# Product-key experts on Trainium2: gates of the listed experts made in list order instead of gathered

## The chip, the cores and the metric

The kernel runs on one core of a Trainium2 chip. A core has TensorE (matrix products, reading SBUF, writing PSUM banks), VectorE, ScalarE and GpSimd for elementwise work, and queues that issue DMA transfers: SyncE's (SP), ScalarE's, and GpSimd's, which issues the indirect ones (row gathers). Each engine runs its own instructions in order and waits on semaphores for the others. The metric is the time of one execution on the device in microseconds (us). The kernel before took 1694.18 us, the median of three runs (1691.24 to 1699.25).

## The reference, cut to what matters

One decoder layer: two kinds of attention, then the expert layer (PEER), then a gated embedding, each followed by a layer norm. The change touches the expert layer only. There are 256 tokens of width 2048, 16,384 experts (numbered ia x 128 + ib), and 8 heads that choose 16 experts each for every token:

```python
cand = (va[..., :, None] + vb[..., None, :]).reshape(t, PEER_HEADS, PEER_TOPK * PEER_TOPK)
cidx = (ia[..., :, None] * PEER_NKEYS + ib[..., None, :]).reshape(...)
top, sel = lax.top_k(cand, PEER_TOPK)
eidx = jnp.take_along_axis(cidx, sel, axis=-1)
gates = jax.nn.softmax(top, axis=-1)
...
    ub = u[eb]
    vbk = v[eb]
    act = jax.nn.gelu(jnp.einsum('thed,td->the', ub, xb).astype(jnp.float32))
    w = (gb * act).astype(xb.dtype)
    return jnp.einsum('the,thed->td', w, vbk)
```

So each token has 128 entries (8 heads x 16), an entry being an expert (ia, ib) with a gate.

## The kernel before, in words

**Sparse and dense tokens.** The first 88 tokens (NSP) are "sparse": for each, the u and the v row of each of its 128 experts is gathered, 176 gathers of 128 rows (1 MB), and VectorE forms the dot products (L1006) and the weighted sums (L1016), in `sparse_work`. The other 168 (NDT) are "dense": for them TensorE multiplies blocks of 128 experts with all tokens at once, and a weight matrix [expert, token] that is zero nearly everywhere holds gate times gelu.

**Two parts of the experts.** Rows ia 0 to 55 (SEG1) are the first part: their u rows are loaded whole in 56 blocks (`u_block`), and gelu of the products stands in A0 and A1, [ib, ia, token]. Rows ia 56 to 127 (SEG2 = 72) are the second part. `list_work` makes for each part a list of the experts that a dense token really uses, in blocks of 128: 24 + 15 = 39 blocks for the first, 30 + 18 = 48 for the second. The first 30 (24) blocks hold experts that only tokens 128 to 255 use (128 columns), the others all 168 columns. The lists are kept as row numbers `idxV` (rows of u and v) and `idxW` (rows of the stored weights). For the second part the u rows are gathered by list (`rows_of`), turned on TensorE (`rows_T`) and multiplied (`rows_mm`): gelu goes to WL, in list order. This is the loop over 48 u blocks.

**The gates.** `gate_work` takes three dense tokens (GB) at a time. VectorE makes two one-hots by `equal` (L714): `ohb` [entry, 128 values of ib] and `eq` [entry, ia]; ScalarE multiplies `eq` by the gate's upper half (`hi`, L1099), VectorE by its lower half (`lo`, L1101). TensorE multiplies `ohb` by `hi` and by `lo` (L1111, L1112): the result in a PSUM bank `ps_G` is the gate of each (ib, ia) for one token. VectorE scales it into place: for the first part into A0 and A1 by multiplication (L1125), for the second as plain gates into the buffer G2 (L1122). `gate_work` is a generator: the loops call `run(work, n)` to let it issue n steps between their own blocks (one step after one-hots, one after products). When all tokens are done, the weights go to DRAM by SP's queue (L289): `s_w0` for the first part, `s_w1` for the second. Row 0 of each is zero, for empty places of the list. The second part's gates begin at the 44th u block and end among the v blocks.

**The v blocks.** `v_fetch` gathers for each listed block two things on GpSimd's queue (L1329): `wc`, the stored weights of its 128 experts (672 bytes a row), and `vf`, their v rows (1 MB). For the second part `weigh` (L1434) multiplies the gathered gates by WL on VectorE. Then 16 products `v_mm` (L1411; an f32 product is two records in the trace) add to six PSUM banks. `vf` has the five slots of the pool `wf` (WF), the same as the u rows had, and `fetched` runs up to four blocks ahead (LEAD). Order: the 39 blocks of the first part, with `half` running two steps of `gate_work` after each half block; then 45 of the second, the last three (STAG) held back and done bank by bank with the layer norm's start. Before the last three a branch `rest` handles experts that didn't fit the lists; it isn't run when all fit.

**Paces.** `gathers(n)` lets `sparse_work` issue n sparse gathers on average after each block: GUL = (1.00, 1.40) after a u block of 128 or 168 columns, GV = (0.66, 0.95) after a v block. Most instructions off TensorE are kept in program order (`keep`); each engine's queue is therefore shared by blocks, gates and sparse sums in the order of issue.

Of the kernel before, what the change touches and what calls it, by code (L numbers as in the profile page):

```python
# [19 lines left out]
P = 128  # L20
# [48 lines left out]
GUL, GV = (1.00, 1.40), (0.66, 0.95)  # L69
# [6 lines left out]
STAG, LEAD, NWC = 3, 4, 8  # L76
# [92 lines left out]
def build(tc, a, out):  # L169
# [464 lines left out]
    m16 = gin.tile([P, 2, P], F16, name="m16")  # L634
    left = gin.tile([P, NIA], F32, name="left")
# [28 lines left out]
    niaT = tkl.tile([P, T], F32, name="niaT")  # L664
    nibT = tkl.tile([P, P], F32, name="nibT")
    zrow = tkl.tile([1, NDT], F32, name="zrow")
    nc.gpsimd.memset(zrow, 0.0)
    for i in range(2):
        nc.gpsimd.dma_start(a[f"s_w{i}"][0:1], zrow[:, None, :].to_broadcast([1, PARTS[i][1], NDT]))
# [180 lines left out]
    def index_T(t):  # L850

        c = slice(t * P, (t + 1) * P)
        for src, dst, neg in ((iaN, iaT, niaT[:, c]), (ibN, ibT, None if t else nibT)):
# [3 lines left out]
            if neg is not None:  # L857
                nc.scalar.mul(neg, ps[:, :P], -1.0)
# [18 lines left out]
    def act_one_hot(dst, pool, neg):  # L877

        d = pool.tile([P, P], F16, name="dist", tag="dist", bufs=1)
        nc.scalar.activation(d, io128, AF.Abs, bias=neg)  # L880
        nc.scalar.activation(dst, d, AF.Relu, bias=1.0, scale=-1.0)
# [6 lines left out]
    def first_flags():  # L888
# [5 lines left out]
        for t0 in range(NSP, P, GB):  # L894
            n = min(GB, P - t0)
            oa, ob = (tkl.tile([P, GB, P], F16, name=nm, tag=nm) for nm in ("oa", "ob"))
            for j in range(n):
                act_one_hot(oa[:, j, :], tkl, niaT[:, t0 + j:t0 + j + 1])
                act_one_hot(ob[:, j, :], tkl, nibT[:, t0 + j:t0 + j + 1])
# [5 lines left out]
    def second_flags(gating, flags):  # L905
# [8 lines left out]
        load(lin, a["c_lin"])  # L914
        iaC = flp.tile([P, SEGX, 2], F16, name="iaC")
# [9 lines left out]
        for i, t0 in enumerate(range(P, T, GB)):  # L925
# [3 lines left out]
            if i % 2:  # L929
                for j in range(n):  # L930
                    act_one_hot(eq[:, j, :], flp, niaT[:, t0 + j:t0 + j + 1])
# [152 lines left out]
    def gate_work(oh, parts, s0, ns, part, fresh):  # L1084

        def one_hot(t0, n):  # L1090
            ohb = oh.tile([P, GB, P], F16, name="ohb", tag="ohb", bufs=OHB)
            eq = oh.tile([P, GB, ns], F16, name="eq", tag="eq", bufs=OHB)
            hi = oh.tile([P, GB, ns], F16, name="hi", tag="hi", bufs=OHB)
            lo = oh.tile([P, GB, ns], F16, name="lo", tag="lo", bufs=OHB)
            equal(eq[:, :n], io128[:, s0:s0 + ns], iaT[:, t0:t0 + n])
            equal(ohb[:, :n], io128, ibT[:, t0:t0 + n])
# [10 lines left out]
        def product(t0, n, ohb, hi, lo):  # L1107
            ps = pbank(pa, "ps_G")
# [4 lines left out]
            return ps  # L1113

        def scale(t0, n, ps):
            g = ps[:, :n * ns].rearrange("p (t a) -> p a t", t=n)
            c0 = 0
            for At in parts:
                dst = At[:, :, t0 - NSP:t0 - NSP + n]
                c1 = c0 + At.shape[1]  # L1120
                if fresh:
# [814 lines left out]
```

## Time and profile before

| | before |
|---|---|
| median of 3 runs | 1694.18 us (1691.24 to 1699.25) |
| the profiled execution | 1699.17 us, its span 1697.4 us |
| instructions | 29309 |
| busy: TensorE matmul, VectorE, ScalarE, GpSimd | 1608.6, 1041.8, 723.3, 697.4 us |
| mean granted TensorE clock | 0.98 of full speed |
| moved by DMA | 528.49 MB, 311 GB/s over the span |

The profile is of one execution. It has the busy time of each engine, the same in stretches of the span, groups of instructions by line (with the idle time ahead of them and what ended it), waits (who waited for whom), and a timeline. A row such as `out<-in` names tiles of the program. "idle before" is the engine's idle time just before an instruction, put down to the event that came last. Matmuls are pipelined, so one's length in the trace is longer than the step from one to the next.

### The profile page before, as it was taken

Reading aid. Unit: us, or ns where it says so; the run is one execution under the profiler, and the core shown is the slowest. Engines: PE = TensorE matmul, PEld = TensorE weight load, DVE = VectorE, ACT = ScalarE, POOL = GpSimd, SP = SyncE. Lnnn points to the kernel's source line nnn. Section 1 sums busy time; section 2 is a strip of 40 time slices with the busy share of each in tenths; the row PEclk is TensorE's granted clock in tenths of the full one; section 3 lists DMA queues with packets and bytes.
Section 4 is the critical chain, followed back from the end, with each engine's and each line's share of the span. In section 5 each row is a group of like instructions: output and inputs, shape, how many; then the busy total and the mean of one; then the engine's idle time right before and its main releaser. Section 6 shows DMA issues by size and latency. Waiting matters only on the chain. (4 is left out here: it accounts for less than half of the span.)

```text
span 1697.4 us, 29309 instructions
## 1 busy us (share of the span) xinstructions
PE 1608.6 (95%) x11162; PEld 1485.0 (87%) x11162; DVE 1041.8 (61%) x2216; ACT 723.3 (43%) x1684; POOL 697.4 (41%) x586
## 2 busy tenths in 40 slices
PE   9999999999999899999999999899977988889998
PEld 7888888877889899999999999889867988889786
DVE  5555488763387897667576666378732444441776
ACT  5677468753111467856366665343300000000542
POOL 0134023202233434211556555448867878862000
PEclk9999999999999999999999999899998999999999
DMA  8544644484997799999899999999998999986561
GB/s 295 193 160 160 237 162 149 153 321 148 332 390 321 300 412 418 370 376 363 345 421 381 358 362 372 367 365 356 394 400 344 401 420 415 414 355 235 183 257 50
DMA packets 93658, 528.49 MB, mean 311 GB/s; under 512 B 13166, under 2 KB 16559, under 8 KB 41371
## 3 DMA queue, kind: packets, MB, share of 16 engines
q0 software_dynamic: 50320, 335.01, 50.2%
q1 hardware_dynamic: 41462, 188.40, 30.1%
q10 hardware_dynamic: 1728, 3.15, 0.5%
q8 instruction: 89, 1.46, 0.3%
q14 instruction: 59, 0.48, 0.1%
HBM read 512.60 MB, written 16.08 MB: 311 GB/s over the span
## 5 line engine op out<-in xcount | busy, mean ns | idle before, releaser
L1411 PE MATMUL ps_v<-wc,vf 128*128 128x128 f32 (+1 forms) x2784 | 373.3, 294 | 51.6 <-DMA vf<-v_rows,idxV 29.3
L1411 PEld LDWEIGHTS ps_v<-wc,vf 128*128 128x128 f32 x2784 | 360.6, 196 | 59.1 <-issue 24.6
L130 DVE TENSOR_TENSOR wl<-wf,wh 128x1024 fp32r<-128x1024 f32 (+1 forms) x199 | 212.7, 1092 | 121.5 <-ACT wh L129 120.0
L1016 DVE SCALAR_TENSOR_TENSOR y<-gb,ew,y 128x2048 f32<-128x2048 f32 x78 | 183.1, 2348 | 167.7 <-DMA gb<-v_rows,eig 167.6
L129 ACT CAST wh<-wf 128x1024 fp32r<-128x1024 f32 (+1 forms) x199 | 172.1, 892 | 267.2 <-DMA wf<-ple_gate 153.3
L220 PE MATMUL ps_u<-XF,wf 128*128 128x168 f32 x1632 | 250.7, 310 | 0.0
L220 PEld LDWEIGHTS ps_u<-XF,wf 128*128 128x128 f32 x1632 | 235.2, 191 | 3.1 <-issue 0.2
L1368 PE MATMUL ps_u<-XF,uT 128*128 128x128 f32 (+1 forms) x1536 | 226.1, 292 | 0.4 <-ACT uT L1362 0.4
L1006 DVE SCALAR_TENSOR_TENSOR gb<-gb,xq 128x2048 f32<-128x2048 f32 x88 | 200.7, 2285 | 31.6 <-DMA gb<-u_rows,eig 30.3
L1040 POOL DMA_INDIRECT gb<-u_rows,eig x88 | 119.6, 1360 | 215.2 <-DVE eqb L714 54.9
L1368 PEld LDWEIGHTS ps_u<-XF,uT 128*128 128x128 f32 x1536 | 203.2, 194 | 1.0 <-ACT uT L1362 0.7
L208 PE MATMUL ps_qk<-X,wh 128*128 128x512 f32 x512 | 185.2, 401 | 0.0
L1040 POOL DMA_INDIRECT gb<-v_rows,eig x88 | 148.1, 1683 | 44.0 <-issue 17.9
L1362 ACT COPY uT<-ps_T 128x512 f32<-128x512 f32 x192 | 111.6, 586 | 98.8 <-PE ps_T L1359 95.7
L210 PE MATMUL ps_qk<-X,wl 128*128 128x256 f32 x512 | 145.7, 285 | 0.0
L1329 POOL DMA_INDIRECT wc<-s_w,idxW x87 | 119.1, 1369 | 47.7 <-issue 22.9
L1099 ACT ACTIVATE hi<-eq,ghf 128x56 f16<-128x56 f16 (+1 forms) x336 | 92.3, 339 | 81.8 <-DVE eq L714 79.9
L1329 POOL DMA_INDIRECT vf<-v_rows,idxV x87 | 103.9, 1194 | 53.9 <-PE ps_v L1411 23.7
L220 PE MATMUL ps_q<-XF,wf 128*128 128x256 f32 x512 | 115.7, 384 | 1.1 <-ACT eb L589 1.1
L208 PEld LDWEIGHTS ps_qk<-X,wh 128*128 128x128 f32 x512 | 96.4, 188 | 22.0 <-issue 1.0
L1359 PE MATMUL ps_T<-ident,uf 128*128 128x128 f32 x768 | 115.5, 276 | 0.0
L1329 POOL DMA_INDIRECT uf<-u_rows,idxV x48 | 68.4, 1426 | 100.4 <-PE ps_T L1359 92.6
(345 smaller groups left out, 2498.4 us busy)
## 6 DMA issues: line engine op xcount, KB each, us to landing
wf<-peer_u SPq DMA_DIRECT2D x51, 1024.0 KB
wf<-w_qk SPq DMA_DIRECT2D x64, 512.0 KB
wf<-w_out SPq DMA_DIRECT2D x32, 512.0 KB
wf<-peer_wq SPq DMA_DIRECT2D x16, 1024.0 KB
wf<-ple_gate SPq DMA_DIRECT2D x16, 1024.0 KB
wf<-w_v SPq DMA_DIRECT2D x16, 512.0 KB
wf<-w_sv SPq DMA_DIRECT2D x15, 512.0 KB
s_w<-G SPq DMA_DIRECT2D x9, 672.0 KB
```

What stands on the lines that cost most here:

```text
L129: self.order(nc.scalar.copy(wh, src))
L130: self.order(nc.vector.tensor_tensor(wl, src, wh.bitcast(F32), op=ALU.subtract))
L208: nc.tensor.matmul(ps, wh[:, j * P:(j + 1) * P], xt[:, dt, :], start=dt == 0, stop=False)
L210: nc.tensor.matmul(ps[:, :T], wl[:, j * P:(j + 1) * P], xt[:, dt, :T], start=False, stop=dt == ND - 1)
L220: nc.tensor.matmul(ps[:, :T - t0], wf[:, dt * P:(dt + 1) * P], xt[:, dt, t0:], start=dt == 0, stop=dt == ND - 1)
L1006: keep(nc.vector.scalar_tensor_tensor(g, g, 1.0, xq[i], op0=ALU.mult, op1=ALU.mult, accum_out=eact[i][:, j:j + 1]))
L1016: keep(nc.vector.scalar_tensor_tensor(ys[i], g, ew[i][:, j:j + 1], ys[i], op0=ALU.mult, op1=ALU.add))
L1040: keep(nc.gpsimd.indirect_dma_start(out=g, out_offset=None, in_=a[kind], in_offset=bass.IndirectOffsetOnAxis(ap=eig[i][:, 0, j:j + 1], axi ...
L1329: keep(nc.gpsimd.indirect_dma_start(out=dst, out_offset=None, in_=src, in_offset=bass.IndirectOffsetOnAxis(ap=idx[:, b:b + 1], axis=0), bo ...
L1359: nc.tensor.transpose(ps[:, j * P:(j + 1) * P], uf[:, (4 * c + j) * P:(4 * c + j + 1) * P], ident)
L1368: nc.tensor.matmul(ps[:, :n], uT[:, j * P:(j + 1) * P], XF[:, d, NSP + c0:NSP + c0 + n], start=d == 0, stop=d == ND - 1)
L1411: return nc.tensor.matmul(o, vf[:, d * P:(d + 1) * P], wc[:, c0:c0 + n], start=False, stop=last and (d % 3 == 2 or d == ND - 1))
```

## The change

The second part's gates are not made in (ib, ia) order, stored and gathered; they are made directly in list order and multiplied into WL, where gelu stands.

- While `gate_work` makes the first part's gates, it also looks up, for all 128 entries of the three tokens, their place in the second part's list. TensorE turns the one-hot `ohb` (one product with a unit matrix, 128 columns, into a bank `ps_turn`), ScalarE copies it to SBUF as f16, and TensorE multiplies it with two small tables `maps` [ib, ia] of block number and place in the block (72 columns each). That gives [entry, ia]; VectorE picks the entry's own ia by comparing with `iaF` and summing (`pick`, one instruction with an accumulator for each token). `decode` splits the place into block and row.
- A second pass of `gate_work` uses row and block in place of ib and ia: 40 tokens with the 18 blocks of 168 columns, then 128 tokens with all 48 blocks, scaled by multiplication into WL. It is run beside the first part's v blocks, and nothing of it beside the u blocks; after the first part's store no step is run there.
- G2, its store `s_w1`, the 48 gathers of `wc` and `weigh` are gone: a v block of the second part multiplies with WL directly.
- Four more slots for v rows (`vx`, NVX) stand where G2 was; every second block among the first eight of a round of nine uses one, for the first part only. `ahead` is 8 blocks until the first part's last five are fetched, then 4 again.
- Paces: GUL (1.10, 1.50), GV (0.62, 0.88).
- The branch `rest` makes the gates of the second part itself (`expert_gates`), from four small tensors stored after the first part's v blocks.

```diff
-GUL, GV = (1.00, 1.40), (0.66, 0.95)
+GUL, GV = (1.10, 1.50), (0.62, 0.88)
...
+    maps = gin.tile([P, 2, SEG2], F16, name="maps")
+    ident16 = gin.tile([P, P], F16, name="ident16")
...
-        for t0 in list(range(NSP, T, GB)) + [None] * OHB:
...
+        made, multiplied, turned, picked = [], None, [], None
+        todo = [(t0, min(GB, t1 - t0), s0, ns, dsts) for first, t1, s0, ns, dsts in runs
+                for t0 in range(first, t1, GB)]
+        for group in todo + [None] * (OHB + 2 * (look is not None)):
+            if group is not None:
+                made.append((group, one_hot(*group[:4])))
             if multiplied:
-                scale(*multiplied)
+                (t0, n, s0, ns, dsts), ps = multiplied
+                scale(t0, n, ns, dsts, ps)
                 multiplied = None
+            if turned and len(turned[-1]) == 3:
+                t0, n, ps = turned.pop()
+                oht = oh.tile([P, GB * P], F16, name="oht", tag="oht", bufs=4)
+                keep(nc.scalar.copy(oht[:, :n * P], ps[:, :n * P]))
+                turned.append((t0, n, oht, True))
+            if picked:
+                look.pick(*picked)
+                picked = None
             yield
...
+            ps = pbank(pa, "ps_G")
+            if ready:
+                group, tiles = made.pop(0)
+                t0, n, _, ns, _ = group
+                product(ps, n, ns, *tiles)
+                multiplied = group, ps
+            if look is not None:
+                if len(turned) > 1 or not ready:
+                    t1, n1, oht, _ = turned.pop(0)
+                    o = ps[:, GB * SEG1:]
+                    look.find(t1, n1, oht, o)
+                    picked = t1, n1, o
+                if ready:
+                    pst = pbank(pa, "ps_turn")
+                    for j in range(n):
+                        nc.tensor.matmul(pst[:, j * P:(j + 1) * P], tiles[0][:, j, :], ident16,
+                                         start=True, stop=True)
+                    turned.append((t0, n, pst))
+            yield
...
+        def find(self, t0, n, oht, ps):
+            for j in range(n):
+                o = ps[:, j * SEG2:(j + 1) * SEG2]
+                for k in range(2):
+                    nc.tensor.matmul(o, oht[:, j * P:(j + 1) * P], maps[:, k], start=not k,
+                                     stop=k == 1)
+
+        def pick(self, t0, n, ps):
+            for j in range(n):
+                junk = self.oh.tile([P, SEG2], F16, name="junk", tag="junk", bufs=2)
+                keep(nc.vector.scalar_tensor_tensor(
+                    junk, io128[:, SEG1:], iaF[:, t0 + j:t0 + j + 1],
+                    ps[:, j * SEG2:(j + 1) * SEG2], op0=ALU.is_equal, op1=ALU.mult,
+                    accum_out=self.pos[:, t0 + j:t0 + j + 1]))
...
+    def all_gates(oh, A0, A1, WL):
+
+        places = Places(lkp, oh)
+        yield from gate_work(oh, iaT, ibT, [(NSP, T, 0, SEG1, ((A0, NSP), (A1, NSP)))], places)
...
+        nonlocal stored
+        stored = True
+        aT, bT = places.decode()
+        yield
+        nA, nB = CAPS[1]
+        WA = WL[:, :nA * P].rearrange("p (b t) -> p b t", t=P)
+        WB = WL[:, nA * P:].rearrange("p (b t) -> p b t", t=NDT)
+        yield from gate_work(oh, aT, bT, [(NSP, P, nA, nB, ((WB, NSP),)),
+                                          (P, T, 0, nA + nB, ((WA, P), (WB, NSP)))])
...
+        k = taken % (WF + NVX)
+        taken += 1
+        if k % 2 and k < 2 * NVX and not i and b < NBLK[0] - WF:
+            vf = vxp.tile([P, D], F32, name="vx", tag="vx", bufs=NVX)
+        else:
+            vf = slot("vf")
+        if i:
+            w = WL_of(b)
+        else:
...
+            rows_of(w, a["s_w"].rearrange("p a t -> (p a) t"), idxW[i], b)
...
-        if b == NBLK[1] - 5:
-            while not run(work, 1):
-                pass
+        if b == NBLK[1] - LEAD:
+            assert stored
             pools.close("a1p", "a0p")
-            g2p = pools.open("g2p", "right", bufs=1)
-            G2 = g2p.tile([P, SEG2, NDT], F32, name="G2")
+            vxp = pools.open("vxp", "right", bufs=1)
             wcp = pools.open("wcp", "right", bufs=1)
-            work = gate_work(ohp, (G2,), *PARTS[1], 1, True)
...
-            if b >= 2 and (c or n > P):
+            if b >= 2 and (c or n > P) and not stored:
                 run(work, 1)
...
-            while order and len(fetched) <= LEAD and (not order[0][0] or done):
-                fetch(wpool)
-            fetched[:3] = [weigh(block) for block in fetched[:3]]
-            i, b, vf, wc, _ = fetched.pop(0)
+            while order and len(fetched) <= (ahead if order[0] < (0, NBLK[0] - WF) else LEAD):
+                fetch()
+            block = fetched.pop(0)
```

More of the change, by code (lines that the diff above doesn't have):

```diff
@@ L856, in index_T @@
             nc.scalar.copy(dst[:, c], ps[:, :P, None].to_broadcast([P, P, 2]))
-            if neg is not None:
-                nc.scalar.mul(neg, ps[:, :P], -1.0)
+            if flat is not None:
+                nc.scalar.copy(flat, ps[:, :P])
             yield
@@ L1105, in one_hot, with product @@
             return ohb, hi, lo
-        def product(t0, n, ohb, hi, lo):
-            ps = pbank(pa, "ps_G")
+        def product(ps, n, ns, ohb, hi, lo):
             for j in range(n):
@@ L1142, in gate_work @@
-        if multiplied:
-            scale(*multiplied)
+            if turned and len(turned[-1]) == 3:
[6 more added lines that the diff above has]
+                picked = None
+            yield
+            ready = made and (len(made) > OHB - 2 or group is None)
@@ L1262, in list_work @@
         idxV[part] = iv
-        idxW[part] = iw
     def run(work, n):
@@ L1460, in build @@
         if b == NBLK[0] - LEAD:
-            while not done:
-                done = run(work, 1)
             more = nc.values_load(total[0:1, 0:1], min_val=0, max_val=NIA * NKEY)
-        v_blocks(1, wcp, half)
-    pools.close("ohp")
-    wcq = pools.open("wcq", "left", bufs=1)
+        v_blocks(1, LEAD + NVX, half)
+    assert done
+    for dst, src in zip(("s_ia", "s_ib", "s_gl"), (iaT, ibT, gl2)):
+        load(a[dst], src[:, NSP:])
+    load(a["s_gh"], ghf[:, NSP:])
+    pools.close("ohp", "lkp")
     for _ in range(LEAD + 1):
-        v_blocks(1, wcq)
-    pools.close("wcp", "g2p", "lsp")
+        v_blocks(1, LEAD)
+    pools.close("wcp", "vxp", "lsp")
     l2 = pools.open("l2", "right", bufs=1)
@@ L1535, in build, with expert_gates @@
         if b == N1 - STAG - 1:
-            fetched[:] = [weigh(block) for block in fetched]
             while not run(sparse, 1):
                 pass
+    def expert_gates(ia0, ia2, ib2, gl, gh):
+        G = spare[2][:, :FBC * NDT].rearrange("p (a t) -> p a t", t=NDT)
+        for t0 in range(0, NDT, 8):
+            t = slice(t0, t0 + 8)
+            eq, hi, lo = (fbp.tile([P, 8, FBC], F16, name=nm, tag=nm) for nm in ("e_", "h_", "l_"))
+            ohb = fbp.tile([P, 8, P], F16, name="o_", tag="o_")
+            equal(eq, io128[:, ia0:ia0 + FBC], ia2[:, t])
+            equal(ohb, io128, ib2[:, t])
+            shape = [P, 8, FBC]
+            keep(nc.vector.tensor_tensor(hi, eq, gh[:, t, None].to_broadcast(shape), op=ALU.mult))
+            keep(nc.vector.tensor_tensor(lo, eq, gl[:, t, 0:1].to_broadcast(shape), op=ALU.mult))
+            ps = pbank(pa, "ps_g")
+            for j in range(8):
+                for k, x in enumerate((hi, lo)):
+                    keep(nc.tensor.matmul(ps[:, j * FBC:(j + 1) * FBC], ohb[:, j], x[:, j],
+                                          start=not k, stop=k == 1))
+            keep(nc.vector.tensor_scalar(
+                G[:, :, t], ps[:, :8 * FBC].rearrange("p (t a) -> p a t", t=8), 1.0 / GSCALE,
+                None, op0=ALU.mult))
+        return G
@@ L1561, in build @@
     pools.close("fbp")
-    held = [weigh(block)[:4] for block in fetched]
+    held = list(fetched)
     assert len(held) == STAG and not order
```

168 lines of the change are left out of this document (93 added, 75 removed).

## The prediction

> **What bounds the kernel now.** I read the stages first, by the busy time in stretches of the span. The columns are the stretch, its length, the busy time of TensorE matmul, weight load, VectorE, ScalarE and GpSimd with instruction counts, then granted clock, DMA share and GB/s.
>
> ```profile
> core 0: us, PE busy (x) PEld busy (x) DVE busy (x) ACT busy (x) POOL busy (x), PEclk, DMA share, GB/s
> ...
> 846.00:1049.00 203.00, 203.00 (x1992) 201.76 (x1988) 135.45 (x330) 126.45 (x343) 119.51 (x72) 1.00 0.97 378
> 1049.00:1085.00 36.00, 36.00 (x275) 35.87 (x274) 13.11 (x8) 14.96 (x29) 12.27 (x10) 1.00 1.01 415
> 1085.00:1135.00 50.00, 39.98 (x281) 37.76 (x280) 33.34 (x59) 20.52 (x61) 30.50 (x21) 0.83 0.91 361
> 1135.00:1241.00 106.00, 101.72 (x1057) 98.78 (x1056) 79.08 (x193) 36.83 (x132) 80.81 (x57) 1.00 0.94 359
> 1241.00:1346.00 105.00, 81.84 (x518) 79.88 (x517) 33.38 (x16) 0.00 (x0) 75.25 (x56) 0.90 0.95 384
> 1346.00:1480.00 134.00, 114.60 (x977) 111.20 (x977) 56.81 (x56) 4.43 (x8) 106.62 (x78) 1.00 1.01 415
> 1480.00:1517.00 37.00, 29.87 (x203) 28.78 (x202) 20.90 (x25) 0.00 (x0) 28.15 (x22) 0.97 1.02 415
> 1517.00:1556.00 39.00, 38.72 (x256) 38.48 (x257) 2.67 (x9) 0.00 (x0) 9.63 (x11) 0.95 0.65 229
> ```
>
> The second part's u blocks run from 828 to 1135, the v blocks from 1135 to 1556: 39 of the first part until 1346, then 45 of the second. While gates are made beside u blocks (846 to 1049), TensorE never idles: it is the bound, VectorE is at two thirds. In the v blocks TensorE is idle for 24 us of 1241 to 1346 and 26 of 1346 to 1517, with the DMA share at 0.95 to 1.02: there the transfers bind. Only after 1517 is TensorE the bound again. The waits of TensorE between 840 and 1560 (total, times, longest) say for what:
>
> ```profile
> PE ps_v L1411 <- DMA vf<-v_rows,idxV: 29.3, 15, 8.6
> PE ps_v L1411 <- DVE wc L1434: 13.2, 7, 7.1
> PE ps_G L1111 <- ACT hi L1099: 9.6, 2, 5.9
> ```
>
> The second wait is the product of gate and value in gathered rows (`weigh`), the third the first gates of the second part. Both go with the change. The timeline of TensorE shows where, and the rates that the sum needs (start, length, operation, count, idle before):
>
> ```profile
> 1094.84 0.22 PE L1111 MATMUL ps_G<-hi,ohb 128*128 128x72 f16 x1 [5.88 <-ACT hi L1099]
> ...
> 1095.80 2.61 PE L1368 MATMUL ps_u<-XF,uT 128*128 128x168 f32 x8 [0.19 <-ACT uT L1362]
> ...
> 1109.35 0.22 PE L1111 MATMUL ps_G<-hi,ohb 128*128 128x72 f16 x1 [3.76 <-ACT hi L1099]
> ...
> 1125.93 1.31 PE L1368 MATMUL ps_u<-XF,uT 128*128 128x168 f32 x8
> ...
> 1139.64 0.20 PE L1111 MATMUL ps_G<-hi,ohb 128*128 128x72 f16 x1
> 1139.67 0.20 PE L1112 MATMUL ps_G<-lo,ohb 128*128 128x72 f16 x1
> ...
> 1139.84 2.03 PE L1411 MATMUL ps_v<-wc,vf 128*128 128x128 f32 x16
> 1141.70 0.20 PE L1111 MATMUL ps_G<-hi,ohb 128*128 128x72 f16 x1
> ```
> ```profile
> 1310.41 34.15 PE L1411 MATMUL ps_v<-wc,vf 128*128 128x168 f32 x224 [8.60 <-DMA vf<-v_rows,idxV]
> ...
> 1516.78 38.95 PE L1411 MATMUL ps_v<-wc,vf 128*128 128x168 f32 x256 [7.05 <-DVE wc L1434]
> ```
>
> An f32 matmul leaves two records, so a v block is 32 of them. 16 records and a gate group take 2.06 us (1139.64 to 1141.70): a 128-column v block with two groups costs 4.12 us, and without the two groups' twelve products at 31 ns about 3.7. A 168-column block costs 38.95 / 8 = 4.87.
>
> **Part 1: u blocks beside the gates and the lookup.** Per token the change adds one f16 matmul of 128 columns (the turn of the one-hot) and two of 72 (the lookup). The 72-column ones lie 31 ns apart above. For 128 columns no f16 row stands; by columns it is 55 ns, between 31 and the 127 ns of one f32 record (2.03 / 16). 168 x 0.055 + 336 x 0.031 = 19.7 us (bounds 15.6 to 32), all on the path, since TensorE is full there. Products of the second part made before 1135 leave this stage: nine or ten groups of six at 31 ns, 1.8 us. Their two stalls leave too: 5.88 + 3.76 us idle, and the slow matmuls behind them, for eight took 2.61 at 1095.80 and 1.31 at 1125.93 (clock 0.83 in that stretch). Four such octets and the transposes between them make some 5 us: 14 us in all.
>
> What ended these stalls on ScalarE was VectorE, whose one-hots stood behind the sparse sums. So VectorE must be costed (mean ns and idle before, in 846 to 1049):
>
> ```profile
> L1016 DVE SCALAR_TENSOR_TENSOR y<-gb,ew,y 128x2048 f32<-128x2048 f32 x15 | 35.2, 2348 | 1.6 <-DMA gb<-v_rows,eig 1.5
> L1125 DVE SCALAR_TENSOR_TENSOR A<-ps_G,A 128x18 f32<-128x18 f32 x111 | 23.4, 253 | 59.7 <-PE ps_G L1112 59.5
> ...
> L1006 DVE DVE_READ_ACCUMULATOR gb<-gb,xq 128x1 f32 x21 | 1.7, 82 | 0.0
> ```
>
> A pick reads 72 PSUM columns and writes out an accumulator: nearest is L1125, 253 ns over 18 and 150 columns, plus 82 ns: up to 0.33 us, 0.25 with the overlap that lets rows of 153 us add up to 135.45 busy. 168 picks are 42 to 55 us. The u pace goes from 1.0 to 1.1, three to four sums more at 2.35 us: 8.5. VectorE then has 186 to 199 us of work in 203 + 20 us. It had 59.7 us of waiting for TensorE to spend. It fits, at 83 to 89%, but the cover is nearly gone: behind a sum that waits for its gather stand one-hots and picks, behind them ScalarE's `hi` and the copies `uT`, and the four PSUM banks are now taken two a group. I charge 5 us (0 to 20). The turned one-hot's copy on ScalarE is priced by
>
> ```profile
> L1362 ACT COPY uT<-ps_T 128x512 f32<-128x512 f32 x192 | 111.6, 586 | 98.8 <-PE ps_T L1359 95.7
> ```
>
> at 0.46 us for 384 of 512 columns: 56 of them, 26 us on 126 of 223: hidden. The stage: 19.7 - 1.8 - 14 + 5 = **9 us longer** (0 to +24).
>
> **Part 2: v blocks of the first part.** Here the change removes the store of the gates and the lookup's wait on it.
>
> ```profile
> 1049.17 4.38 SPq L289 DMA_DIRECT2D s_w<-A  x8
> 1237.30 10.46 SPq L289 DMA_DIRECT2D s_w<-G  x9
> ```
> ```profile
> s_w<-G SPq DMA_DIRECT2D x9, 672.0 KB
> ```
>
> Nine stores of 672 KB are 6.2 MB, 15 us at 415 GB/s, just where the 168-column blocks begin: the 15 of them took 105 us, and 7 took 34.15 once the data came. Gates now run on beside the blocks: 57 groups at two a block, to the 29th. With 48 columns a product is no dearer than the old one of 72. TensorE's sum is 24 x 4.12 + 15 x 4.87 + 9 x 0.19 + 2 (opening the banks) = 176 us. The transfers: 36 blocks of v rows (three of the four fetched early have landed), 1.049 MB each, 36 gathers of 0.086 MB, and 24 x 0.62 + 15 x 0.88 = 28 sparse gathers of 1.049: 70 MB, 169 us at 415, 180 at 390. The two nearly meet, and what the four added slots are worth is that they need not meet block by block. I take 182 for the old 211: **29 us shorter** (20 to 35). The first weights' store (s_w<-A) keeps its place, as the last scaling of A falls in the 37th u block as before, and so does the wait on GpSimd for it:
>
> ```profile
> 1087.81 2.29 POOL L1329 DMA_INDIRECT wc<-s_w,idxW  x1 [7.16 <-DMA s_w<-A]
> ```
>
> That is 45 us ahead of the v blocks, which cover it; the sparse gathers queued behind it held VectorE's one-hots in the two stalls above, and no one-hots are left there. A wait is added: the first scaling into WL needs the last u block's gelu. Only VectorE stands there, for one group. Nothing for these.
>
> **Part 3: v blocks of the second part.** No gather of weights, no `weigh` on VectorE, a lower sparse pace.
>
> ```profile
> L1040 POOL DMA_INDIRECT gb<-v_rows,eig x88 | 148.1, 1683 | 44.0 <-issue 17.9 <-DVE eq L714 9.1 <-DMA gb<-v_rows,eig 5.6
> ...
> L1040 POOL DMA_INDIRECT gb<-u_rows,eig x22 | 39.4, 1791 | 6.6 <-issue 3.8 <-DVE A L1125 1.8 <-DVE eq L714 0.9
> ```
>
> These rows run from 828: of 176 sparse gathers 66 lie before it. The u blocks then make 30 x 1.1 + 18 x 1.5 = 60 (before 55.2), the first part 28, and 22 are left: 30 blocks at 0.62 and 4 at 0.88. So 34 blocks share the transfers, (34 + 22) x 1.049 = 58.7 MB or 141 us at 415 GB/s; three more bring it to the 37 of the old stretch 1346 to 1517: 156. TensorE's own work in it is 30 x 3.7 + 7 x 4.87 + 5 (transposes, the natural sums) = 150. The old stretch took 171, with the 7.05 us in which the last weighing stood behind the last sums. I take 158: **13 us shorter** (8 to 18). The last eight blocks stay TensorE's. Buffers are as before, since no added slot serves the second part.
>
> The Trainium skill (DMA: Bandwidth & Descriptors, Bandwidth) holds that loads from HBM are bound at some 358 GB/s for each core. The trace disagrees: 415 over 171 us. By 358 the two DMA sums would be 196 and 164 us.
>
> **Rest.** The lookup tables cost two small VectorE operations ahead of 828, where `neg` copies only change sign; the gates' new work in the branch `rest` isn't run if the lists hold all; four small stores after the first part's blocks lie on SP's queue, empty there. Zero, plus or minus 2.
>
> **Sum**: +9 - 29 - 13 = -33 us. The profiled execution took 1699.17 us (span 1697.4): 1666. It stands 5 us above the median of the runs, 1694.18; against that, **1661 us**. From the ends of the terms: -53 to -4, 1641 to 1690.
>
> **Rivals.** *VectorE takes the u stage.* If a pick costs much more, VectorE's in-order queue sets the pace and TensorE waits at each product. Slower by 8.5 us overall needs the stretch of 203 us to reach 269: 135 + 8.5 + 12 waiting for gathers + 168 p = 269, p = 0.68 us. At 0.8 it gives 290: 62 us more than the 228 of the forecast, 1723. For: 83 to 89% use in one in-order queue. Against: twice the nearest row. 0.07.
>
> *The rate falls.* With TensorE no longer idling, the same queues may not hold 415: 359 and 361 GB/s stand in the rows at 1135 and 1085. At 360 the first part takes 195, the second's stretch 163 + 15 = 178: -16 and +7, with +9 no change: 1694. Against it: those stretches had slack elsewhere, not full transfers (0.91, 0.94). The rule on HBM above would end here. 0.09.
>
> *Lookahead is not had.* The sparse gathers stand in the same queue, and a late one holds VectorE, the one-hots and so the gate products: the v blocks can run no further ahead than the three sparse buffers in flight allow (3 / 0.62, five blocks, not nine). Then the first part goes at the transfers' pace block by block, (1.049 x 1.62 + 0.086) / 0.415 = 4.3 us and with 1.88 gathers 5.0: 24 x 4.3 + 15 x 5.0 + 10 for the start = 188, -23, in all -27: 1667. 0.22. *The change doesn't do what it says* (gates not done by the 35th block, so that v blocks wait for them) is out by the count of 29.5 blocks: 0.01, counted with the second rival.
>
> **How the numbers follow.** The forecast has 0.61, and a measurement here tells some 0.5%, 8.5 us, from no change. Forecast and third rival lie below 1685.7 but for a tail. Faster 0.83, same 0.10, slower 0.07. Range 1641 (all terms good) to 1686; beyond it the first two rivals.
>
> **What would show it.** Right: TensorE still near full in the gate stretch, now about 225 us long, with VectorE above 0.8; no idle time near the end of the u blocks; the first part's 168-column blocks at 5 us each; no row of DVE `wc` (L1434) and no 7 us stop before the last blocks; `wc` gathers 39, not 87; DMA at 1.0 and 415 GB/s through the v blocks. Wrong: TensorE waiting for ScalarE `hi` or VectorE picks by tens of us, or v blocks still waiting for `vf` as long as now at the same share.

## The result, and the profile after

On one chip the changed kernel took 1667.01 us (median of 4 runs, 1664.92 to 1669.44) and the kernel before 1693.05 (4 runs): a ratio of 0.984 [0.9811, 0.9869], 26 us less. The forecast was 1661, in a range of 1641 to 1686. The profiled execution took 1664.92 us, its span 1663.1.

Stage by stage, from the two profiled executions. A stage begins with its first transpose of u rows, its first product with gathered weights, and its first product with a block of the second part; the last of the three ends at the first transpose of the natural sums (L1552, L1486 before):

| us | u blocks | v, first part | v, second part | behind the v blocks |
|---|---|---|---|---|
| before | 307 | 210 | 215 | 136 |
| after | 311 | 184 | 211 | 134 |
| difference | +3.8 | -26.2 | -4.7 | -2.4 |
| forecast | +9 | -29 | -13 | 0 |

The three stages give -27.1 us, about what the medians differ by. The rest of the 34 us between the two profiled executions lies ahead of the u blocks (they begin at 823.7 instead of 828.5; over all the profiles of this case at 820.3 to 828.5) and behind the v blocks, where the change does next to nothing. The profiled execution of before stood 6 us above its median, that of after 2 us below.

The busy time in stretches, after (stretch, length, TensorE matmul, weight load, VectorE, ScalarE, GpSimd, granted clock, DMA share, GB/s). The u blocks end near 1135, the first part's v blocks at 1318.6:

```profile
core 0: us, PE busy (x) PEld busy (x) DVE busy (x) ACT busy (x) POOL busy (x), PEclk, DMA share, GB/s
841.00:1065.00 224.00, 224.00 (x2498) 222.28 (x2496) 175.46 (x659) 145.21 (x401) 99.24 (x76) 1.00 0.96 369
1065.00:1115.00 50.00, 50.00 (x388) 49.59 (x387) 20.88 (x26) 19.73 (x40) 26.59 (x19) 1.00 0.93 364
1115.00:1135.00 20.00, 17.59 (x119) 15.83 (x119) 3.02 (x2) 5.21 (x11) 15.73 (x15) 1.00 0.96 362
1135.00:1240.00 105.00, 104.97 (x992) 103.67 (x991) 51.69 (x123) 18.06 (x76) 77.56 (x58) 1.00 1.00 404
1240.00:1300.00 60.00, 60.00 (x534) 59.46 (x533) 36.29 (x125) 17.81 (x69) 39.59 (x28) 1.00 0.96 369
1300.00:1319.00 19.00, 4.59 (x70) 3.54 (x69) 19.00 (x52) 6.17 (x24) 13.00 (x8) 0.64 0.95 342
1319.00:1452.00 133.00, 117.40 (x962) 115.84 (x962) 60.95 (x27) 4.43 (x8) 76.31 (x56) 0.92 1.01 416
1452.00:1489.00 37.00, 37.00 (x260) 36.52 (x259) 21.86 (x22) 0.00 (x0) 12.04 (x12) 1.00 1.01 414
1489.00:1530.00 41.00, 40.85 (x289) 40.62 (x287) 3.55 (x6) 2.18 (x4) 5.93 (x6) 1.00 0.72 241
```

The first row is the gates with the lookup: 224 us, TensorE full, VectorE at 78%. The fourth has the first part's v blocks at full speed, the sixth 19 us in which TensorE did 4.6 us of work and VectorE was never idle. TensorE's waits between 823 and 1540 (total, times, longest):

```profile
PE ps_v L1489 <- DMA vf<-v_rows,idxV: 15.5, 6, 5.0
PE ps_G L1107 <- DVE eq L715: 8.7, 5, 2.8
PE ps_G L1107 <- DVE WL L1116: 3.1, 3, 2.1
PE ps_T L1439 <- DMA uf<-u_rows,idxV: 2.4, 1, 2.4
```

The wait for `vf` went from 29.3 to 15.5 us; the waits for L1434 and for the first gates in the u stage are gone, as forecast. New are the second and third row, and both lie in that sixth stretch. TensorE's timeline there (start, length, operation, count, idle before) shows that only gate products were left, each group waiting for its one-hots or for a bank:

```profile
1303.19 0.18 PE L1107 MATMUL ps_G<-hi,ohb 128*128 128x48 f16 x1 [2.29 <-DVE eq L715]
...
1307.16 0.20 PE L1107 MATMUL ps_G<-hi,ohb 128*128 128x48 f16 x1 [2.81 <-DVE eq L715]
...
1311.09 0.20 PE L1107 MATMUL ps_G<-hi,ohb 128*128 128x48 f16 x1 [2.70 <-DVE eq L715]
...
1318.64 1.65 PE L1489 MATMUL ps_v<-WL,vf 128*128 128x128 f32 x6 [2.27 <-DVE WL L1116]
```

The first product of the second part comes at 1318.64, behind the last scaling into WL. Why the gates came so late shows VectorE's timeline:

```profile
1129.39 2.35 DVE L1018 SCALAR_TENSOR_TENSOR y<-gb,ew,y 128x2048 f32<-128x2048 f32 x1 [28.09 <-DMA gb<-v_rows,eig]
...
1176.88 2.35 DVE L1018 SCALAR_TENSOR_TENSOR y<-gb,ew,y 128x2048 f32<-128x2048 f32 x1 [8.32 <-DMA gb<-v_rows,eig]
1179.15 0.18 DVE L715 TENSOR_TENSOR eq<-io,blkT 128x54 f16<-128x54 f16 x1
```

L1018 is a sparse sum, L715 the second pass's first one-hots. VectorE waited 28 us for the rows of one sum, took that and eight more one by one as their rows landed, and came to the one-hots at 1179, when the v blocks had run for 44 us. And those rows landed late because of GpSimd's queue:

```profile
1088.36 2.31 POOL L1400 DMA_INDIRECT uf<-u_rows,idxV  x1 [4.60 <-PE ps_T L1439]
1101.33 1.00 POOL L1400 DMA_INDIRECT wc<-s_w,idxW  x1 [10.66 <-issue]
...
1118.26 1.00 POOL L1400 DMA_INDIRECT wc<-s_w,idxW  x1 [0.30 <-issue]
1119.56 0.99 POOL L1400 DMA_INDIRECT uf<-u_rows,idxV  x1 [0.31 <-issue]
1120.86 0.96 POOL L1042 DMA_INDIRECT gb<-v_rows,eig  x1 [0.30 <-issue]
```

Behind the u rows issued at 1088, GpSimd stood 10.66 us at the first gather of stored weights, whose rows the store of A had still to bring to DRAM. Then came ten weight gathers and four v gathers into the added slots, and only at 1120 the last u rows and the next sparse gather. In the program all ten weight gathers stand behind the last u rows. The profile names no releaser for the wait (it says "issue"); the profile of before named the store for the same one.

### The profile page after: what moved, and what is told of

The parts are those of the page before. It is cut to its first block, busy times and chain, and to the rows that moved or that the text cites. A ratio compares the mean times of both kernels' runs of the same rounds, so it can differ in the third digit from the quotient of the medians.

```text
span 1663.1 us, 30575 instructions
## 1 busy us (share of the span) xinstructions
PE 1610.7 (97%) x11666; PEld 1491.9 (90%) x11666; DVE 1056.0 (63%) x2557; ACT 735.7 (44%) x1740; POOL 603.1 (36%) x538
## 5 line engine op out<-in xcount | busy, mean ns | idle before, releaser
L1018 DVE SCALAR_TENSOR_TENSOR y<-gb,ew,y 128x2048 f32<-128x2048 f32 x78 | 183.2, 2349 | 145.7 <-DMA gb<-v_rows,eig 144.5
L1489 PE MATMUL ps_v<-WL,vf 128*128 128x128 f32 (+1 forms) x1536 | 204.9, 297 | 18.0 <-DMA vf<-v_rows,idxV 15.5
L1448 PE MATMUL ps_u<-XF,uT 128*128 128x128 f32 (+1 forms) x1536 | 220.2, 288 | 0.0
L1489 PEld LDWEIGHTS ps_v<-WL,vf 128*128 128x128 f32 x1536 | 201.4, 200 | 20.4 <-DMA vf<-v_rows,idxV 17.2
L1448 PEld LDWEIGHTS ps_u<-XF,uT 128*128 128x128 f32 x1536 | 199.1, 191 | 0.7
L1042 POOL DMA_INDIRECT gb<-u_rows,eig x88 | 105.3, 1196 | 210.0 <-DVE eqb L715 42.7
L1042 POOL DMA_INDIRECT gb<-v_rows,eig x88 | 131.5, 1494 | 53.4 <-issue 20.4
L1096 ACT ACTIVATE hi<-eq,ghf 128x56 f16<-128x56 f16 (+2 forms) x336 | 87.0, 325 | 141.4 <-DVE eq L715 137.8
L1400 POOL DMA_INDIRECT vf<-v_rows,idxV x72 | 92.0, 1278 | 113.0 <-PE ps_v L1489 85.8
L221 PEld LDWEIGHTS ps_q<-XF,wf 128*128 128x128 f32 x512 | 96.1, 191 | 13.2 <-ACT eb L590 0.9
L1400 POOL DMA_INDIRECT uf<-u_rows,idxV x48 | 60.3, 1257 | 123.2 <-PE ps_T L1439 112.6
```

The source lines that it names most:

```text
L221: nc.tensor.matmul(ps[:, :T - t0], wf[:, dt * P:(dt + 1) * P], xt[:, dt, t0:], start=dt == 0, stop=dt == ND - 1)
L1018: keep(nc.vector.scalar_tensor_tensor(ys[i], g, ew[i][:, j:j + 1], ys[i], op0=ALU.mult, op1=ALU.add))
L1042: keep(nc.gpsimd.indirect_dma_start(out=g, out_offset=None, in_=a[kind], in_offset=bass.IndirectOffsetOnAxis(ap=eig[i][:, 0, j:j + 1], axi ...
L1400: keep(nc.gpsimd.indirect_dma_start(out=dst, out_offset=None, in_=src, in_offset=bass.IndirectOffsetOnAxis(ap=idx[:, b:b + 1], axis=0), bo ...
L1448: nc.tensor.matmul(ps[:, :n], uT[:, j * P:(j + 1) * P], XF[:, d, NSP + c0:NSP + c0 + n], start=d == 0, stop=d == ND - 1)
L1489: return nc.tensor.matmul(o, vf[:, d * P:(d + 1) * P], w, start=False, stop=last and (d % 3 == 2 or d == ND - 1))
```

## The experiments

The kernels ran in three groups, each beside the kernel before on its own chip: it took 1694.24 us in the first (rows 1 to 4 of the table), 1702.03 in the second (rows 5 to 8), 1695.02 in the third (rows 9 to 12). Stages as above, rounded:

| us | u | v first | v second | median | ratio to before |
|---|---|---|---|---|---|
| no gather of gates | 305 | 195 | 205 | 1666.44 | 0.9827 [0.9809, 0.9844] |
| neither gather nor store | 306 | 179 | 206 | 1651.19 | 0.9741 [0.9722, 0.9761] |
| no lookup | 292 | 191 | 212 | 1652.11 | 0.9749 [0.9731, 0.9768] |
| lead of 4 | 313 | 184 | 211 | 1666.79 | 0.9833 [0.9816, 0.9849] |
| quiet | 328 | 181 | 209 | 1675.92 | 0.9839 [0.9799, 0.9879] |
| quiet once stored | 325 | 183 | 214 | 1682.16 | 0.9874 [0.9834, 0.9914] |
| no slots | 324 | 194 | 202 | 1675.22 | 0.9837 [0.9795, 0.988] |
| double pick | 328 | 193 | 212 | 1691.49 | 0.9934 [0.9912, 0.9957] |
| changed kernel again | 313 | 184 | 211 | 1666.95 | 0.9831 [0.9817, 0.9844] |
| five weight buffers, no slots | 308 | 196 | 201 | 1659.95 | 0.9786 [0.9769, 0.9802] |
| five weight buffers, slots | 310 | 189 | 200 | 1654.38 | 0.9759 [0.9746, 0.9773] |
| old paces | 316 | 179 | 213 | 1662.95 | 0.9807 [0.9794, 0.9821] |

**No gather of gates** (from the kernel before; the gates are left out of the second part's blocks, but still made and stored):

```diff
+        if i:
+            rows_of(vf, a["v_rows"], idxV[i], b)
+            return vf, WL_of(b)
...
-        if i and raw:
+        if False:
```

> The kernel before, with the second part's gathers of stored weights and their multiplication on VectorE left out: these v blocks multiply with gelu alone (the gates are missing from them). Gates, store, slots and paces stay. If the gathers and the waits on them carry the gain: the first part's v blocks (210 us) fall to 185 to 195, since nothing waits for the store any more though its 6.2 MB still move, the second's (210) to about 197, 1665 in all. If the gain came from the added slots or the paces: within 8 us of 1693.

27.8 us faster than before.

**Neither gather nor store** (the same, and the second part's gates are not stored either):

```diff
-                load(a[f"s_w{part}"][1:, a0:a0 + n], At[:, c:c + n])
+                if not part:
+                    load(a[f"s_w{part}"][1:, a0:a0 + n], At[:, c:c + n])
```

> As the one before, and the store of the second part's gates is left out too. If the store's bytes count where transfers bind: 10 to 15 us below the kernel with the store, first part's v blocks at 176 to 182 us, in all about 1652. If only the wait on the store counted: the same time as with the store.

Another 15.2 us, and all of it in the first part's v blocks (195 to 179): the store's 6.2 MB at 415 GB/s are 15 us. Together what the change removes is worth 43 us, one more than the 42 that the forecast had for the two v stages.

**No lookup** (from the changed kernel; turn, find and pick are left out, and every entry gets the same constant place):

```diff
-        yield from gate_work(..., places)
+        nc.vector.memset(places.pos, 300.0)
+        yield from gate_work(...)
```

> The changed kernel without the lookup (no turned one-hots, no products with the tables, no picks; every place is a constant, so the second part's gates are wrong). If TensorE is the bound beside the gates, as the prediction has it: the u stage of 311 us falls by 17 to 20 us to about 292, and the whole by as much, 1649. If VectorE's picks were the bound: by more than 30. If the lookup lies in idle time: by less than 5.

14.7 us faster than the next kernel, which is the changed one in all but name. In the u stage alone the lookup costs 311.2 - 291.9 = 19.3 us against the profile after (21 against the next kernel): the forecast's 19.7 us of TensorE time, and hardly more. Part of it comes back in the v blocks, which take 403 us here and 394 there: at the end of the first part TensorE waits 14.5 us for one-hots, where the changed kernel waits 8.7. The gain and the cost add up: 43 us for what is removed, less 14.7 for the lookup, are 28, and the next kernel is 27.5 us faster than the kernel before.

GpSimd's timeline of this run bears on the reading of the queue above:

```profile
1062.36 0.93 POOL L1042 DMA_INDIRECT gb<-v_rows,eig  x1 [0.30 <-issue]
...
1077.27 2.17 POOL L1401 DMA_INDIRECT wc<-s_w,idxW  x1 [2.59 <-issue]
...
1099.04 0.95 POOL L1042 DMA_INDIRECT gb<-v_rows,eig  x1 [0.31 <-issue]
```

The first weight gather waits 2.59 us here, not 10.66. Still no sparse gather is issued for 37 us (41 in the changed kernel), and the one-hots start 49 us into the v blocks. So the wait for the store doesn't make them late by itself; what both runs have is the ten weight gathers and four v gathers ahead of the sparse ones.

**Lead of 4** (`ahead` not raised for the added slots):

```diff
-        v_blocks(1, LEAD + NVX, half)
+        v_blocks(1, LEAD, half)
```

> The changed kernel with four blocks of lookahead everywhere: the four added slots stay, but no fetch runs further ahead than before. If the slots carry the gain: 15 us slower or more, 1682 and up, with waits for vf back in the first part. If the early fetches delay the sparse gathers and with them the one-hots of the second pass (first one-hot 45 us after the v blocks begin, TensorE idle or on gates alone for 18 us at the end of the first part): the first one-hot comes earlier, that stop shrinks by 10 us or more, and the whole is equal or up to 10 us faster.

The same time and the same stages. Its instruction lists are those of the changed kernel, engine by engine: the order of GpSimd's transfers isn't the program's. A transfer is moved ahead as far as free buffers allow (ten weight gathers with ten buffers, five with five, below), and how far `fetch` is called ahead decides nothing. So this run is a repeat, and says that buffers are the handle.

**Quiet** (no sparse gathers after the last four u blocks) and **quiet once stored** (none after u blocks once the first part's weights are stored):

```diff
-        gathers(GUL[n > P])
+        else:
+            gathers(GUL[n > P])
```
```diff
-        gathers(GUL[n > P])
+        if not stored:
+            gathers(GUL[n > P])
```

> The changed kernel without sparse gathers after the last four u blocks: six sums fewer stand on VectorE's queue ahead of the second pass's one-hots (5 instead of 11); the six move to the second part's v blocks. If these sums, waiting for their gathers, are what starts the one-hots 45 us late: the first one-hot comes 20 to 30 us after the v blocks begin, the stop of 18 us at the end of the first part shrinks to under 10, and the whole is 3 to 10 us faster (1657 to 1664). If the late start has another cause (the last gelu, TensorE's order): no change in the stop, and the six gathers cost up to 15 us in the second part.

> The same, with no sparse gather from the moment that the first part's weights are stored: no sum stands between the lookup's decoding and the second pass's one-hots. By the first theory: one-hots ahead of the v blocks, no stop at the first part's end, first part at 166 to 172 us instead of 184; ten or eleven gathers more after 1135, 26 us of transfers, so that the second part loses what is gained: 1655 to 1668. By the second: as the changed kernel, plus up to 26 us.

These two make the gates early. In the second, VectorE's timeline and TensorE's waits between 820 and 1545:

```profile
1089.00 2.35 DVE L1018 SCALAR_TENSOR_TENSOR y<-gb,ew,y 128x2048 f32<-128x2048 f32 x1 [5.69 <-DMA gb<-v_rows,eig]
...
1092.60 0.18 DVE L715 TENSOR_TENSOR eq<-io,blkT 128x54 f16<-128x54 f16 x1
```

```profile
PE ps_v L1490 <- DMA vf<-v_rows,idxV: 12.1, 7, 2.8
PE ps_y L1553 <- DVE XF L1504: 10.7, 1, 10.7
```

The one-hots start at 1092.6 instead of 1179.1, and no product waits for them. The first part takes 183 us all the same, not the 166 to 172 that I expected, and the second 214, with 10.7 us at its end behind sparse sums: the gathers that were held back are paid there. In "quiet" the one-hots start at 1139.6, with 181 and 209 us, and it is 6 us faster than the other. The 19 us stop at the end of the first part is thus not 19 us of loss: without it the first part is no more than 3 us shorter (181 and 183 us, for 184). In the second kernel TensorE was busy for 177 of the 183 us, so little was left to win; and while TensorE stood in the changed kernel, the v rows for the next blocks landed at 342 GB/s.

**No slots** (the four added v slots are taken out, ten buffers for gathered weights kept) and **double pick** (each pick done twice):

```diff
-STAG, LEAD, NVX = 3, 4, 4
+STAG, LEAD, NVX = 3, 4, 0
...
-            w = wcp.tile([P, NDT], F32, name="wc", tag="wc", bufs=WF + NVX + 1)
+            w = wcp.tile([P, NDT], F32, name="wc", tag="wc", bufs=WF + 5)
```
```diff
-            for j in range(n):
+            for j in [*range(n), *range(n)]:
```

> The changed kernel without the four added slots (five for v rows, as before). If the slots are worth what the prediction says (first part's blocks need not meet the transfers one by one): 4 to 15 us slower, waits for vf back in the first part. If the early fetches into them hold the sparse gathers back, which then fall into the second part (30 there instead of the 22 of the pace): equal or up to 10 us faster.

> The changed kernel with every pick done twice (the second writes the same value again). 168 times 0.283 + 0.082 us is 61 us more on VectorE in the u stage, which stood at 175 of 224 us busy. By the prediction's count for the rival, slower only once the work exceeds the stretch: 175 + 50 to 61 is 225 to 236 of 224, so the stage grows by 5 to 20 us and TensorE begins to wait for picks or one-hots. If the queue's waits already set the stage: by 40 or more. If VectorE has more room than its busy time says: by less than 3.

Without the slots the time is that of "quiet" in the same group. The changed kernel isn't in this group; against its stages in the others the first part is 10 us longer without slots, the second 9 shorter, and the v blocks take 396 us for 394 to 395. So beside ten weight buffers I see no worth in the slots. The double pick is 16 us above "quiet" and "no slots", but doesn't cost it where it stands:

```profile
841.00:950.00 109.00, 109.00 (x1236) 108.35 (x1235) 96.91 (x458) 71.29 (x200) 47.60 (x37) 1.00 0.98 388
950.00:1065.00 115.00, 115.00 (x1259) 113.73 (x1258) 108.57 (x509) 72.44 (x201) 48.02 (x39) 1.00 0.91 339
```

TensorE is full in the whole stretch, as it was, and VectorE's work rose from 175 to 205 us of 224, by 0.19 us for each of the 162 added picks. The loss shows later: the v blocks take 405 us, against 390 to 396 in the other three of the group, and TensorE waits 9.3 us for one-hots, against 0.2 to 3.1. But the changed kernel waits 8.7 us for them with v blocks of 394, so these waits don't say what the loss comes from. That is open.

All four kernels of this group show something that no other run does. In "no slots", ScalarE's and TensorE's timelines:

```profile
1107.52 0.58 ACT L1442 COPY uT<-ps_T 128x512 f32<-128x512 f32 x1 [2.12 <-issue]
1121.06 0.58 ACT L1442 COPY uT<-ps_T 128x512 f32<-128x512 f32 x1 [12.96 <-remote]
```

```profile
1109.40 1.47 PE L1439 MATMUL ps_T<-ident,uf 128*128 128x128 f32 x12
1121.70 2.61 PE L1448 MATMUL ps_u<-XF,uT 128*128 128x168 f32 x8 [10.82 <-ACT uT L1442]
```

By TensorE's records the transposes were done by 1111. ScalarE copied them at 1121, 13 us after its last copy, with nothing between; the profile puts the wait down to "remote" and shows no event. Meanwhile TensorE stood 10.8 us. The u stages of this group are 324 to 328 us in large part for that reason (TensorE stood for 4.3 to 10.8 us near 1115 in the four), and their totals are compared with each other only.

**The changed kernel again**:

> The changed kernel once more, so that the other kernels of this group have it on their own chip. On the first chip it stood at 0.984 of the kernel before, with a u stage of 311 us and v blocks of 394 us. Four variants on a second chip, with the same program up to the end of the gates, all had u stages of 324 to 329 us, in which ScalarE stood still for 11 to 13 us near 1110 with no record of a cause. If that belongs to the chip, the changed kernel shows it too when it runs there, and the kernel before pays as well; if it belongs to those variants, this run shows 311 again on any chip. Expected: a ratio of 0.981 to 0.987.

The same ratio, the same stages, and no such stop on this chip.

**Five weight buffers**, without and with the slots:

```diff
-STAG, LEAD, NVX = 3, 4, 4
+STAG, LEAD, NVX = 3, 4, 0
...
-            w = wcp.tile([P, NDT], F32, name="wc", tag="wc", bufs=WF + NVX + 1)
+            w = wcp.tile([P, NDT], F32, name="wc", tag="wc", bufs=LEAD + 1)
```

(the second has only the last two lines)

> No added slots, and five buffers for gathered weights as in the kernel before, instead of ten. Then five weight gathers stand ahead of the last gather of u rows on GpSimd's queue instead of ten and four v gathers, and the sparse gathers are spread more evenly: 35 instead of 20 stand among the 39 weight gathers, 26 instead of 41 behind them. If the queue's order costs time (little to transfer from 1100 to 1116 at 204 to 330 GB/s, 30 instead of 22 sparse gathers for the second part), it is 5 to 9 us faster than the changed kernel on the same chip. If only the bytes count, which are the same in both, it is within 3 us. If the slots are worth something, it is slower by more than 3 us.

> The four added slots kept, with five buffers for gathered weights. Five weight gathers and three v gathers stand ahead of the last gather of u rows; 33 sparse gathers stand among the weight gathers, 28 behind them. If the queue's order costs time, it is 4 to 8 us faster than the changed kernel on the same chip; by the bytes alone within 3 us. If the slots are worth something beside that, it is faster than the kernel with five buffers and no slots by over 3 us; I expect the two within 2 us of each other.

By the medians 7.0 and 12.6 us faster than the changed kernel on that chip; by the stages of the profiled executions 1.6 and 9.5. GpSimd's timeline in the second:

```profile
1100.23 1.00 POOL L1400 DMA_INDIRECT wc<-s_w,idxW  x1 [12.68 <-ACT uT L1442]
...
1111.98 0.99 POOL L1400 DMA_INDIRECT uf<-u_rows,idxV  x1 [0.30 <-PE ps_T L1439]
1113.27 0.95 POOL L1042 DMA_INDIRECT gb<-v_rows,eig  x1 [0.30 <-DMA wc<-s_w,idxW]
```

The first weight gather still waits, 12.68 us (put down to a copy of ScalarE's this time). But five weight gathers follow instead of ten, the last u rows go at 1112 instead of 1120, and the sparse gathers behind them too. The stretches, cut as above, of the kernel with slots, to 1452:

```profile
1135.00:1240.00 105.00, 91.91 (x921) 90.35 (x921) 68.81 (x184) 26.51 (x109) 85.01 (x55) 0.95 0.98 390
1240.00:1300.00 60.00, 58.00 (x509) 57.09 (x508) 42.18 (x117) 15.46 (x59) 47.13 (x38) 1.00 1.01 409
1300.00:1319.00 19.00, 19.00 (x136) 19.00 (x135) 9.70 (x5) 0.00 (x0) 15.72 (x10) 1.00 0.96 365
1319.00:1452.00 133.00, 122.81 (x1040) 120.29 (x1040) 54.46 (x30) 4.43 (x8) 65.48 (x55) 0.99 1.01 420
```

From 1240 to 1300 the transfers run at 409 GB/s instead of 369, and the stop at 1300 is gone. The sparse gathers in the second part's stretch, after and here (GpSimd's group, count, busy, mean):

```profile
L1042 POOL DMA_INDIRECT gb<-v_rows,eig x30 | 41.1, 1371 | 19.1 <-issue 7.9 <-DVE gb L1018 3.7 <-DMA gb<-v_rows,eig 3.4
```

```profile
L1042 POOL DMA_INDIRECT gb<-v_rows,eig x24 | 27.6, 1152 | 8.9 <-issue 6.7 <-DMA vf<-v_rows,idxV 1.9 <-DMA gb<-v_rows,eig 0.3
```

30 against 24. Six gathers of 1.049 MB at 415 GB/s are 15 us; the second part is 11 us shorter (200 for 211). The first, which takes the six (32 for 26), is 5 us longer, and TensorE waits 7.5 us in it for gathered weights, where with ten buffers it waited for none. With this order the slots are worth 5.6 us (1659.95 to 1654.38; the intervals of the ratios overlap between 0.9769 and 0.9773). This is the fastest of the kernels that leave nothing out, 0.9759 of the kernel before.

Over all the runs without the second part's weight gathers, the sparse gathers issued in the second part go with its time: 22 of them and 201 or 202 us (the two kernels without slots), 24 and 200 (this one), 25 and 205 or 206 (the first two kernels of the table), 30 and 211 to 212 (the changed kernel, its repeats, no lookup, double pick), 33 or 35 and 209 to 214 (old paces, the two quiet ones). Ten weight buffers without slots leave 22 as well: it is the two together that leave 30.

**Old paces**:

```diff
-GUL, GV = (1.10, 1.50), (0.62, 0.88)
+GUL, GV = (1.00, 1.40), (0.66, 0.95)
```

> The changed kernel with the sparse paces of the kernel before (1.0 and 1.4 a u block, 0.66 and 0.95 a v block). Three fewer sparse gathers then go before the first weight gather, two more behind the last. If the v blocks are bound by what is left to transfer, 2 to 3 gathers of 1.049 MB at 415 GB/s make it 5 to 8 us slower than the changed kernel. If the u stage pays as much for a sum as the v blocks save by it, it is within 3 us.

By the medians 4.0 us faster than the changed kernel, with intervals that overlap between 0.9817 and 0.9821; by the stages of the profiled executions the same (708.2 and 707.8 us). The u stage is 3.5 us longer, the first part 4.5 us shorter, with the one-hots at 1161 instead of 1177, and the second pays 1.4 us. So the raised paces bring nothing, and what I expected of the bytes left over, 5 to 8 us, isn't there. I read it so, which no run separates: a sum asked for early, whose rows can't be had early, holds VectorE instead.

## Why the forecast was right, and where it was not

The sign and the sum were right for the reasons given, within 6 us. Between the two profiled executions the difference is even the forecast's (-34 for -33), but that is luck: 7 us of it lie outside the three stages, in the "Rest" that the forecast put at 0, plus or minus 2, and in the stages it promised 6 us too much. By its steps:

**Part 1 (+9, measured +3.8).** TensorE's 19.7 us for the lookup are confirmed by the run without it (19.3). That leaves -15.5 for the two stalls and the moved products, forecast as -15.8. The step that failed is the last: "I charge 5 us (0 to 20)" for VectorE's queue, and next to nothing came. The rows for the pick and for VectorE's remaining idle time, 841 to 1065:

```profile
L1179 DVE SCALAR_TENSOR_TENSOR junk<-io,iaF,ps_G 128x72 f16<-128x72 f16 x162 | 37.9, 283 | 0.0
L1116 DVE SCALAR_TENSOR_TENSOR A<-ps_G,A 128x18 f32<-128x18 f32 x112 | 23.6, 253 | 49.6 <-PE ps_G L1173 45.0 <-PE ps_G L1108 4.5
...
L1179 DVE DVE_READ_ACCUMULATOR junk<-io,iaF,ps_G 128x1 f32 x162 | 13.3, 82 | 0.0
```

A pick's two records are 283 + 82 = 365 ns, above the 0.25 to 0.33 us of the forecast, but they overlap with their neighbours: VectorE was busy 175 us and not 186 to 199, with the four more sums that were forecast. By the double pick, a pick adds 0.19 us. VectorE still waited 49.6 us for TensorE, and its share was 0.78, a little below the 0.8 that the forecast named as a sign. Another 30 us of picks changed nothing beside the u blocks, so the rival *VectorE takes the u stage* was far off.

**Part 2 (-29, measured -26.2).** The store's 15 us are confirmed (195.4 to 178.8 in the first part without it). TensorE's sum of 176 us is about right: it was busy for 169 us of this part in the changed kernel and for 177 in "quiet once stored". (A small slip: by its row, TensorE's idle time of 1241 to 1346 before is 23 us, not 24.) The blocks ran at TensorE's rate until 1300, 105.0 busy of 105 us in the fourth stretch, at 404 GB/s, as the slots and the sum of 176 us would have it. Then came the stop, and with it 183.8 us, near the 182 forecast. The step that failed is a sentence: "no one-hots are left there [...] Nothing for these". The sparse gathers queued behind the weight gathers and the wait for `s_w<-A` did hold VectorE and with it the second pass, 44 us into the v blocks. The "count of 29.5 blocks" by which gates end beside the 29th block counted from the first block on; they started after some twelve. That the v blocks could run on with all their slots hid most of it.

**Part 3 (-13, measured -4.7).** Here lies most of the error. The step: "The u blocks then make 30 x 1.1 + 18 x 1.5 = 60 [...], and 22 are left". The u stage made 54, where the kernel before had made 57:

```profile
L1042 POOL DMA_INDIRECT gb<-v_rows,eig x32 | 47.9, 1498 | 20.4 <-DVE y L1018 12.2 <-issue 7.6 <-DMA uf<-u_rows,idxV 0.3
L1042 POOL DMA_INDIRECT gb<-u_rows,eig x22 | 29.5, 1342 | 8.4 <-issue 4.4 <-DVE gb L1008 2.2 <-DVE junk L1179 1.2
```

A pace only says how many are asked for. Six of the 60, as many as the last four u blocks ask for, were not yet issued when the v blocks began, and the first part made 26 where the forecast had 28, instead of catching up. So 30 were left for the second part instead of 22: 8 x 1.049 MB at 415 GB/s, 20 us of transfers more than the sum had, of which 8 us show in the time. The step that failed is thus the count of the gathers and not the time that follows from it: in the two kernels that left 22, the ones without slots, the second part took 201 and 202 us, and the forecast's is 215 - 13 = 202. (Their first part took 196 and 194.) With five weight buffers and the slots the u stage made 54 again, but the first part made 32, and with 24 left the second part came out at 200 us, 15.7 below the kernel before: the 13 us were there to be had.

**The rivals.** *The rate falls* is out: 404 GB/s with TensorE full, and 416 over the 133 us from 1319 on. (Over the whole first part it was 386, not the 415 of the forecast's signs.) The 358 GB/s that the prediction took from the Trainium skill (DMA: Bandwidth & Descriptors, Bandwidth) are there a core's share when both cores of an HBM domain stream; for one core alone the same section has 425 GB/s at 16 MB. This kernel runs on one core, and its 404 to 420 GB/s are near the second figure. *Lookahead is not had* gave 1667, the measured time, and had the right first link, a late sparse gather that holds VectorE and the gate products. Its price was wrong: the v blocks didn't fall to the transfers' pace block by block (no wait for `vf` in the fourth and fifth stretches), and the time was lost at the end of the first part and in the second. That its figure is the measured one is chance: 8 us not gained in the second part and 3 in the first, less the 5 not needed in the u stage.

That the ten weight buffers, beside the slots, are a cause of the loss in the second part is shown by the kernel that changes these buffers only: 24 sparse gathers left for 30, and 9.5 us less by the stages. How much of its 12.6 us by the medians is fewer gathers left over, and how much the earlier one-hots (1171 for 1177), isn't separated. The wait for the store doesn't decide it alone: with 2.59 us of it, in the run without the lookup, 30 were left too. Why the u stage issues 51 to 56 whatever the buffers and the pace, and not 60, no run shows.

## What to carry to other kernels

Before crediting a raised pace or an added buffer, read the queue that has to issue it: what waits at its head, what will be moved ahead of it when buffers come free, and which in-order engine waits for what stands behind. More buffers for a cheap transfer can cost time, as the ten did here beside the added slots: they let it pass ahead of the transfers that are waited for. And a count of the gathers by stage, before and after, tells where one that wasn't made early is paid.

## What the runs showed of the hardware

ScalarE stood still for 8 to 13 us near 1110 in all four kernels of the second group, and in none of the ten others profiled here. The kernel before was 7 us slower in that group too. Whether that belongs to the chip, or to the moment, is open: the kernel before wasn't profiled there.

A stop of TensorE costs more than its length: in the 19 us at 1300 the granted clock was 0.64, and 0.92 over the next 133 us (where the 15.5 us of waits for `vf` lie too); after the 10.8 us at 1111 (no slots), eight records took 2.61 us at a granted clock of 0.50, where eight took 1.31 at 1.00 from 1130 on.
